# Attention inside a decoder trunk: scores of one query tile ahead of the values of the tile before, and the division by the row sum folded into the transposing product

## The chip, the cores and the metric

The kernel runs on one core of a Trainium2 chip. The metric is the device time of one execution in microseconds, median of several runs. The core has a matrix engine (TensorE: PE for its products, PEld for the loading of its stationary operands), VectorE (DVE), ScalarE (ACT), GpSimd (POOL) and a queue that issues transfers (SyncE, SP).

## What is computed

Two layers of a decoder trunk on 512 tokens of width 1024, in float32: a gated feed-forward half step, a mixer, a second half step, each between a modulated normalisation and a normalised residual. The mixer has three branches beside each other: an attention with 8 heads of 64, a gated linear recurrence (16 blocks of 64) and a matrix-state recurrence (8 heads of 64, called RWKV here). The change lies in the attention branch:

```python
def _fox_attention(q, k, v, f_logit, f_bias):
    log_f = jax.nn.log_sigmoid((f_logit + f_bias).astype(jnp.float32))
    F = jnp.cumsum(log_f, axis=1).transpose(0, 2, 1)
    ...
    def block(args):                       # 128 queries at a time
        qi, Fi, pi = args
        s = jnp.einsum('bhqd,bhkd->bhqk', qi, k).astype(jnp.float32) * scale
        s = s + (Fi[..., :, None] - F[..., None, :])
        s = jnp.where(kpos[None, :] <= pi[:, None], s, -jnp.inf)
        p = jax.nn.softmax(s, axis=-1).astype(v.dtype)
        return jnp.einsum('bhqk,bhkd->bhqd', p, v)
```

## The kernel before

All tokens fit on the chip, so every stage holds 512 columns of tokens and streams weights past them. A weight arrives by one transfer (`raw`, L182), ScalarE rounds it to its leading part (`hi`, L194), GpSimd or VectorE subtracts to get the rest (`lo`, L196), and `mm3` makes three products of the parts (L201 to L203). In the mixer's branch stage (`mix_branches`) GpSimd takes the subtraction.

That stage weaves four generators together. `fox` (attention, four pairs of heads) and then `lru` yield a cost at each step; while the summed cost rises, steps of `rwkv` are taken at a rate of 4 x 30.5 over the whole, gate products (`gates`, L1156 to L1164) up to 22, and background work for the next sub-layer. The steps of `rwkv` are written with a priority 16 instructions ahead of their place. The framework then makes each engine's list: it goes through the program in the order written, by a model of time, and gives an engine the earliest instruction that the model has ready. On the chip an engine takes its list in that order, so an instruction whose input comes later than modelled holds up everything behind it on its engine.

`fox_pair` handles two heads (`hh`) for all tokens. It first makes q, k and v of the pair (L1019 to L1041), then loops over four query tiles `i` of 128 queries. The keys of tile `i` are the first 128(i+1) tokens. For each head: GpSimd adds the causal mask (`fm`, L1052); two products give the scores `sc` (L1054, L1055); VectorE scales, adds the forget bias and keeps the maximum (L1058, and L1062 for the earlier keys), then negates it (`nm`, L1066); ScalarE exponentiates with a row sum (L1068); VectorE takes the reciprocal of the sum (L1069) and multiplies the row by it (L1070). Then, for each head, TensorE transposes `e` block by block into `pt` (L1077), VectorE (head 0, L1082) or ScalarE (head 1, L1080) copies that to `et`, and products with `vs` give the output `po` (L1089), which ScalarE stores to `aout` (L1091). Per pair these are 8 rows of scores and 20 blocks to transpose; over 4 pairs and 2 layers, 64 and 160.

Buffers that matter: `e` has 2 (the tag is shared with `vf` and two tiles of the prelude), `et` 2, and the scores, the transposed blocks, the output and the transposed v share the 3 banks of tag `s` in PSUM.

Of the kernel before, what the change touches and what calls it, by code (L numbers as in the profile page):

```python
# [9 lines left out]
F32 = mybir.dt.float32  # L10
F32R = mybir.dt.float32r
AF = mybir.ActivationFunctionType
ALU = mybir.AluOpType
PSUM = bass.MemoryType.PSUM

P = 128
S = 512
D = 1024
DFF = 2816
NT = S // P  # L20
# [8 lines left out]
H = 8  # L29
# [30 lines left out]
class Trunk:  # L60
# [915 lines left out]
    def fox_prelude(self, l, ap):  # L976

        nc = self.nc
        (w,) = self.raw(self.w_in[:, :, 1536:1568])
        room = ap.tile([P, S], F32, tag="et", bufs=2, name=self.nm("room"))  # L980
        fb = room[:, 5 * NT * H : 5 * NT * H + H]
        nc.scalar.dma_start(out=fb, in_=self.a["fox_f_bias"][l : l + 1, :].broadcast_to([P, H]))
        ps = self.ps("s")

        for k0 in (0, 4):
            for h in (self.hhi, self.hlo):
                for g in range(4):
                    nc.tensor.matmul(out=ps[32 * g : 32 * g + 32, :], lhsT=w[:, k0 + g, :], rhs=h[:, k0 + g, :].bitcast(F32),
                                     start=k0 == 0 and h is self.hhi, stop=k0 == 4 and h is self.hlo, skip_group_check=True)
        yf = ap.tile([P, S], F32, tag="e", bufs=2, name=self.nm("yf"))  # L990
        nc.vector.tensor_copy(yf, ps)
        yield 1.5
        ps = self.ps("s")
        for t in range(NT):
            nc.tensor.matmul(out=ps[:, t * H : (t + 1) * H], lhsT=yf[:, t * P : (t + 1) * P], rhs=self.fold[:, 0:H], start=True, stop=True)
        T = lambda n: room[:, "yezwp".index(n) * NT * H :][:, 0 : NT * H].rearrange("p (t h) -> p t h", t=NT)
        y = T("y")
        nc.vector.tensor_tensor(out=y, in0=ps[:, 0 : NT * H].rearrange("p (t h) -> p t h", t=NT),
                                in1=fb.unsqueeze(1).to_broadcast([P, NT, H]), op=ALU.add)
        sp = self.softplus_neg(y, T)  # L1000
        yield 0.8
        ps = self.ps("s")
        for t in range(NT):
            nc.tensor.transpose(ps[0:H, t * P : (t + 1) * P], sp[:, t, :], self.ident)
        nF = ap.tile([P, S], F32, tag="e", bufs=2, name=self.nm("nF"))[0:H, :]
        ones = self.ones[0:H, :].to_broadcast([H, S])
        nc.vector.tensor_tensor_scan(out=nF, data0=ones, data1=ps[0:H, :], initial=0.0, op0=ALU.mult, op1=ALU.add)
        nc.vector.tensor_scalar(out=nF, in0=nF, scalar1=8.0, scalar2=None, op0=ALU.mult)
        self.nF = self.dp.tile([H, S], F32, tag="nF", bufs=2, name=self.nm("nFd"))
        nc.sync.dma_start(out=self.nF, in_=nF)  # L1010
        yield 0.7

    def fox_pair(self, l, p, ap):


        nc = self.nc
        mm = nc.tensor.matmul


        qs = ap.tile([P, 2, S], F32R, tag="q", bufs=1, name=self.nm("q"))  # L1020
        ks = ap.tile([P, 2, S], F32R, tag="k", bufs=1, name=self.nm("k"))
        kl = self.kl
        vs = ap.tile([P, NT, P], F32, tag="v", bufs=1, name=self.nm("v"))
        ps = self.gemm("aq", p)
        for hh, r in enumerate(ROWS):
            nc.scalar.activation(qs[r, hh, :], ps[r], AF.Copy)
            nc.vector.tensor_tensor(out=qs[ROWS[1 - hh], hh, :], in0=ps[r], in1=qs[r, hh, :].bitcast(F32), op=ALU.subtract)
        yield 5.2
        ps = self.gemm("ak", p)
        for hh, r in enumerate(ROWS):  # L1030
            nc.scalar.activation(ks[r, hh, :], ps[r], AF.Copy)
            nc.vector.tensor_tensor(out=kl[r, hh, :], in0=ps[r], in1=ks[r, hh, :].bitcast(F32), op=ALU.subtract)
            nc.gpsimd.tensor_copy(ks[ROWS[1 - hh], hh, :], ks[r, hh, :])
        yield 5.2
        vf = ap.tile([P, S], F32, tag="e", bufs=2, name=self.nm("vf"))
        nc.vector.tensor_copy(vf, self.gemm("av", p))
        pv = self.ps("s")
        for t in range(NT):
            nc.tensor.transpose(pv[:, t * P : (t + 1) * P], vf[:, t * P : (t + 1) * P], self.ident)
        nc.scalar.activation(vs.rearrange("p t c -> p (t c)"), pv, AF.Copy)  # L1040
        yield 5.2  # L1041
        fbs = []
        for hh in range(2):
            fbs.append(ap.tile([P, S], F32, tag="fb", bufs=2, name=self.nm("fb")))
            nc.sync.dma_start(out=fbs[hh], in_=self.nF[2 * p + hh : 2 * p + hh + 1, :].broadcast_to([P, S]))
        yield 0.9
        for i in range(NT):
            n = i * P
            es = []
            for hh, fb in enumerate(fbs):  # L1050
                fm = ap.tile([P, P], F32, tag="fm", bufs=2, name=self.nm("fm"))
                nc.gpsimd.tensor_tensor(out=fm, in0=fb[:, n : n + P], in1=self.causal, op=ALU.add)  # L1052
                sc = self.ps("s")
                mm(out=sc[:, 0 : n + P], lhsT=qs[:, hh, n : n + P], rhs=ks[:, hh, 0 : n + P], start=True, stop=False)  # L1054
                mm(out=sc[:, 0 : n + P], lhsT=qs[:, hh, n : n + P], rhs=kl[:, hh, 0 : n + P], start=False, stop=True)  # L1055
                e = ap.tile([P, S], F32, tag="e", bufs=2, name=self.nm("e"))
                m = self.sp.tile([P, 2], F32, tag="mx", name=self.nm("mx"))
                nc.vector.tensor_tensor_reduce(out=e[:, n : n + P], in0=sc[:, n : n + P], in1=fm, scale=0.125,  # L1058
                                               scalar=-3e38, op0=ALU.add, op1=ALU.max, accum_out=m[:, 0:1])
                last = m[:, 0:1]  # L1060
                if i:
                    nc.vector.tensor_tensor_reduce(out=e[:, 0:n], in0=sc[:, 0:n], in1=fb[:, 0:n], scale=0.125,  # L1062
                                                   scalar=last, op0=ALU.add, op1=ALU.max, accum_out=m[:, 1:2])
                    last = m[:, 1:2]
                nm = self.sp.tile([P, 1], F32, tag="nmx", name=self.nm("nmx"))
                nc.vector.tensor_scalar(out=nm, in0=last, scalar1=-1.0, scalar2=None, op0=ALU.mult)  # L1066
                rs = self.sp.tile([P, 1], F32, tag="rsum", name=self.nm("rsum"))
                nc.scalar.activation(e[:, 0 : n + P], e[:, 0 : n + P], AF.Exp, bias=nm, accum_out=rs)  # L1068
                nc.vector.reciprocal(rs, rs)  # L1069
                nc.vector.tensor_scalar(out=e[:, 0 : n + P], in0=e[:, 0 : n + P], scalar1=rs, scalar2=None, op0=ALU.mult)  # L1070
                es.append(e)
                yield 0.2 * (i + 1)
            ets = []
            for hh, e in enumerate(es):
                pt = self.ps("s")
                for j in range(i + 1):
                    nc.tensor.transpose(pt[:, j * P : (j + 1) * P], e[:, j * P : (j + 1) * P], self.ident)  # L1077
                et = ap.tile([P, S], F32, tag="et", bufs=2, name=self.nm("et"))
                if hh:
                    nc.scalar.activation(et[:, 0 : n + P], pt[:, 0 : n + P], AF.Copy)  # L1080
                else:
                    nc.vector.tensor_copy(et[:, 0 : n + P], pt[:, 0 : n + P])  # L1082
                ets.append(et)
                yield 0.1 * (i + 1)

            po = self.ps("s")
            for j in range(i + 1):
                for hh, et in enumerate(ets):
                    mm(out=po[64 * hh : 64 * hh + 64, 0:P], lhsT=vs[:, j, hh * 64 : hh * 64 + 64],  # L1089
                       rhs=et[:, j * P : (j + 1) * P], start=j == 0, stop=j == i, skip_group_check=True)  # L1090
            nc.scalar.activation(self.aout[:, p, n : n + P], po[:, 0:P], AF.Copy)  # L1091
            yield 0.25 * (i + 1)

    def mix_branches(self, l):

# [405 lines left out]
```

## Time and profile before

| | |
|---|---|
| median of 3 runs | 3092.01 us (3088.25 to 3103.22) |
| the profiled execution, its own time | 3098.59 us |
| its span, first to last instruction | 3096.5 us |
| PE busy | 2931.2 us, 95% |
| DVE busy | 1880.0 us, 61% |
| ACT busy | 1142.2 us, 37% |
| POOL busy | 554.8 us, 18% |
| mean granted clock of PE | 0.983 |

The attention's query tiles lie from 502 to 782 us of the span in layer 0 and from 2034 to 2313 us in layer 1; between them and after them lie the recurrences, the merge and the feed-forward steps. In the profile, "idle before" an instruction is the time in which its engine did nothing, and the name behind the arrow is what ended that. A row with x4 has four instructions of one line in one piece.

### The profile page before, as it was taken

How to read it: one execution, taken by the hardware profiler on the slowest of the kernel's cores; microseconds unless marked ns; L12 is line 12 of the kernel's file. 1: busy time of each engine (PE TensorE's matmuls, PEld its weight loads, DVE VectorE, ACT ScalarE, POOL GpSimd, SP SyncE). 2: the span in 40 equal slices, each digit the busy share in tenths (PEclk: the TensorE clock that was granted, in tenths of full speed). 3: DMA queues.
4: the chain of work that ended last, by engine and by line, in shares of the span. 5: the costliest groups of instructions: out<-in, count | busy, mean ns of one | idle time of the engine just before them, and what ended most of it. 6: DMA issues, size and time to landing. Idle time of an engine off the chain costs nothing. (4 is left out here: it accounts for less than half of the span.)

```text
span 3096.5 us, 39351 instructions
## 1 busy us (share of the span) xinstructions
PE 2931.2 (95%) x15330; PEld 2338.4 (76%) x15330; DVE 1880.0 (61%) x3534; ACT 1142.2 (37%) x1699; POOL 554.8 (18%) x379
## 2 busy tenths in 40 slices
PE   7999998998989998999999999889989899999998
PEld 5888886676766788888888887767666677788887
DVE  6755567666785656565656546667676756654435
ACT  4322253332545635222342214433335554342212
POOL 0000142333232013000130002423333320230000
PEclk9999999999999999999999999999999999999999
DMA  8634333333342463434434424433333424632221
GB/s 280 224 109 146 115 117 101 88 87 102 94 113 67 139 203 118 139 122 143 129 117 136 133 92 145 127 99 93 88 90 93 107 73 143 204 116 96 89 68 62
DMA packets 389402, 372.17 MB, mean 120 GB/s; under 512 B 54964, under 2 KB 318544, under 8 KB 389216
## 3 DMA queue, kind: packets, MB, share of 16 engines
q1 hardware_dynamic: 377048, 350.14, 37.0%
q10 hardware_dynamic: 12168, 19.53, 1.7%
q8 instruction: 120, 1.97, 0.3%
q14 instruction: 66, 0.54, 0.1%
HBM read 347.54 MB, written 22.09 MB: 119 GB/s over the span
## 5 line engine op out<-in xcount | busy, mean ns | idle before, releaser
L194 ACT ACTIVATE hi<-raw 128x1024 fp32r<-128x1024 f32 (+1 forms) x460 | 469.2, 1028 | 1248.9 <-PE pg L202 501.3
L196 POOL TENSOR_TENSOR lo<-raw,hi 128x1024 fp32r<-128x1024 f32 x164 | 408.0, 2490 | 1692.1 <-ACT hi L194 1639.2
L201 PE MATMUL pg<-hhi,hi 128*128 128x512 f32 (+1 forms) x1744 | 680.4, 393 | 13.7 <-DVE ks L645 3.7
L202 PE MATMUL pg<-hlo,hi 128*128 128x512 f32 (+1 forms) x1744 | 673.5, 389 | 2.9 <-DVE nm L343 2.9
L203 PE MATMUL pg<-hhi,lo 128*128 128x512 f32 (+1 forms) x1744 | 674.8, 391 | 0.0
L196 DVE TENSOR_TENSOR lo<-raw,hi 128x1024 fp32r<-128x1024 f32 (+1 forms) x296 | 342.5, 1165 | 301.3 <-ACT hi L194 296.1
L201 PEld LDWEIGHTS pg<-hhi,hi 128*128 128x128 f32 x1744 | 330.9, 190 | 86.9 <-issue 10.5
L203 PEld LDWEIGHTS pg<-hhi,lo 128*128 128x128 f32 x1744 | 330.6, 190 | 66.5 <-issue 2.1
L202 PEld LDWEIGHTS pg<-hlo,hi 128*128 128x128 f32 x1744 | 331.2, 190 | 65.3 <-issue 4.7
L202 PE MATMUL pr<-hlo,hi 128*128 128x512 f32 (+1 forms) x816 | 300.4, 368 | 5.1 <-DVE nm L343 2.9
L201 PE MATMUL pr<-hhi,hi 128*128 128x512 f32 (+1 forms) x816 | 301.5, 370 | 2.2 <-ACT hhi L397 2.2
L203 PE MATMUL pr<-hhi,lo 128*128 128x512 f32 (+1 forms) x816 | 300.7, 369 | 0.0
L284 DVE SCALAR_TENSOR_TENSOR acc<-raw,cact,acc 128x512 f32<-128x512 f32 x224 | 187.7, 838 | 48.7 <-DMA raw<-in_ada_w_dram 44.3
L202 PEld LDWEIGHTS pr<-hlo,hi 128*128 128x128 f32 x816 | 155.0, 190 | 34.2 <-issue 7.4
L201 PEld LDWEIGHTS pr<-hhi,hi 128*128 128x128 f32 x816 | 155.1, 190 | 28.1 <-ACT hhi L397 2.6
L203 PEld LDWEIGHTS pr<-hhi,lo 128*128 128x128 f32 x816 | 155.2, 190 | 27.4
L352 POOL TENSOR_TENSOR rstd<-var,mhalf 128x1 f32<-128x1 f32 x48 | 30.2, 630 | 470.5 <-DVE var L351 461.9
L201 PE MATMUL ps<-hi,ahi 128*128 128x512 f32 x264 | 103.5, 392 | 0.0
L203 PE MATMUL ps<-hi,alo 128*128 128x512 f32 x264 | 103.3, 391 | 0.0
L202 PE MATMUL ps<-lo,ahi 128*128 128x512 f32 x264 | 103.1, 391 | 0.0
L480 DVE TENSOR_TENSOR su<-pg,su 128x512 f32<-128x512 f32 x42 | 28.9, 689 | 115.2 <-PE pg L203 115.1
L480 DVE TENSOR_TENSOR su<-pr,su 128x512 f32<-128x512 f32 x42 | 29.0, 690 | 110.0 <-PE pr L203 105.9
(443 smaller groups left out, 4956.9 us busy)
## 6 DMA issues: line engine op xcount, KB each, us to landing
raw<-in_ffn_up_dram SPq DMA_DIRECT2D x70, 1024.0 KB
raw<-in_w_in_dram SPq DMA_DIRECT2D x132, 512.0 KB
raw<-in_ada_w_dram SPq DMA_DIRECT2D x64, 1024.0 KB
raw<-in_ffn_down_dram SPq DMA_DIRECT2D x40, 1024.0 KB
raw<-in_ffn_up_dram SPq DMA_DIRECT2D x36, 512.0 KB
gspill<-gate ACTq DMA_DIRECT2D x48, 256.0 KB
gate<-gspill SPq DMA_DIRECT2D x48, 256.0 KB
ada<-in_ada_w_dram SPq DMA_DIRECT2D x16, 512.0 KB
```

What stands on the lines that cost most here:

```text
L194: self.nc.scalar.activation(hi, v, AF.Copy)
L196: eng.tensor_tensor(out=lo, in0=v, in1=hi.bitcast(F32), op=ALU.subtract)
L201: mm(out=ps, lhsT=lhi, rhs=rhi, start=start, stop=False, **kw)
L202: mm(out=ps, lhsT=lhi, rhs=rlo, start=False, stop=False, **kw)
L203: return mm(out=ps, lhsT=llo, rhs=rhi, start=False, stop=stop, **kw).ins
L284: nc.vector.scalar_tensor_tensor(out=acc, in0=r[:, i, :], scalar=c, in1=acc, op0=ALU.mult, op1=ALU.add)
L352: nc.gpsimd.tensor_tensor(out=r, in0=v, in1=self.mhalf, op=ALU.pow)
L480: nc.vector.tensor_tensor(out=su, in0=pss[1], in1=su, op=ALU.mult)
```

## The change

`fox_pair`'s loop over tiles is cut in two generators. `scores(i)` does the work up to the reciprocal, and `values(i)` the rest; they are called in the order scores 0, scores 1, values 0, scores 2, values 1, scores 3, values 2, values 3. The costs that are yielded are the same, in the new order. VectorE no longer multiplies the row by the reciprocal. In its place ScalarE makes a diagonal matrix `dg` from the identity, scaled by the reciprocals, and the transposition of a block by the identity becomes a product of the block with `dg`. `e` gets 4 buffers in place of 2, and `dg` has 4 (6 KB more in each partition).

```diff
-        yf = ap.tile([P, S], F32, tag="e", bufs=2, name=self.nm("yf"))
+        yf = ap.tile([P, S], F32, tag="e", bufs=4, name=self.nm("yf"))
...
-        for i in range(NT):
+        def scores(i, es):
+
             n = i * P
-            es = []
             for hh, fb in enumerate(fbs):
...
                 rs = self.sp.tile([P, 1], F32, tag="rsum", name=self.nm("rsum"))
                 nc.scalar.activation(e[:, 0 : n + P], e[:, 0 : n + P], AF.Exp, bias=nm, accum_out=rs)
                 nc.vector.reciprocal(rs, rs)
-                nc.vector.tensor_scalar(out=e[:, 0 : n + P], in0=e[:, 0 : n + P], scalar1=rs, scalar2=None, op0=ALU.mult)
-                es.append(e)
+                dg = ap.tile([P, P], F32, tag="dg", bufs=4, name=self.nm("dg"))
+                nc.scalar.activation(dg, self.ident, AF.Copy, scale=rs)
+                es.append((e, dg))
                 yield 0.2 * (i + 1)
+
+        def values(i, es):
+
+            n = i * P
             ets = []
-            for hh, e in enumerate(es):
+            for hh, (e, dg) in enumerate(es):
                 pt = self.ps("s")
                 for j in range(i + 1):
-                    nc.tensor.transpose(pt[:, j * P : (j + 1) * P], e[:, j * P : (j + 1) * P], self.ident)
+                    mm(out=pt[:, j * P : (j + 1) * P], lhsT=e[:, j * P : (j + 1) * P], rhs=dg, start=True, stop=True)
...
+        es = [[] for _ in range(NT)]
+        yield from scores(0, es[0])
+        for i in range(NT):
+            if i + 1 < NT:
+                yield from scores(i + 1, es[i + 1])
+            yield from values(i, es[i])
```

## Rows read from the trace of the kernel before

**Rows 1.** The page, part 1: busy time, share of the span, instructions.

```profile
PE 2931.2 (95%) x15330; PEld 2338.4 (76%) x15330; DVE 1880.0 (61%) x3534; ACT 1142.2 (37%) x1699; POOL 554.8 (18%) x379
```

**Rows 2.** Two stretches with attention: PE, PEld, DVE, ACT, POOL busy; clock, DMA.

```profile
477.00:800.00 323.00, 288.70 (x1743) 216.19 (x1742) 223.56 (x625) 107.01 (x216) 98.77 (x79) 0.96 0.34 94
2009.00:2335.00 326.00, 293.46 (x1773) 219.91 (x1773) 228.43 (x628) 112.20 (x224) 101.12 (x79) 0.97 0.35 96
```

**Rows 3.** Waits of PE, 477 to 800: total us, times, longest.

```profile
PE ps L1077 <- DVE e L1070: 14.2, 9, 2.8
PE pr L822 <- DVE room L619: 4.4, 1, 4.4
...
PE ps L1089 <- DVE T L866: 1.0, 1, 1.0
```

**Rows 4.** Waits of PE, 2009 to 2335.

```profile
PE ps L1077 <- DVE e L1070: 11.3, 8, 2.8
```

**Rows 5.** Timeline, layer 0, first pair, tiles 0 and 1: start us, us, engine.

```profile
502.40 0.28 PE L1055 MATMUL ps<-kl,q 128*128 128x128 f32 x1
...
503.28 2.41 POOL L196 TENSOR_TENSOR lo<-raw,hi 128x1024 fp32r<-128x1024 f32 x1 [5.47 <-ACT hi L194]
...
503.49 2.28 DVE L866 TENSOR_TENSOR T<-Y 64x60 f32<-64x60 f32 x1
...
503.88 0.19 ACT L1068 ACTIVATION_READ_ACCUMULATOR e<-e,nmx 128x1 f32 x1
...
506.81 0.15 DVE L1069 RECIPROCAL rsum<-rsum 128x1 f32<-128x1 f32 x1
...
508.25 0.33 PE L1077 MATMUL ps<-ident,e 128*128 128x128 f32 x1 [2.75 <-DVE e L1070]
...
511.76 0.51 PE L1054 MATMUL ps<-k,q 128*128 128x256 f32 x1
```

**Rows 6.** Timeline of one multiplication by the reciprocal and the transposition behind it.

```profile
531.10 2.35 POOL L196 TENSOR_TENSOR lo<-raw,hi 128x1024 fp32r<-128x1024 f32 x1
...
531.36 2.38 DVE L1070 TENSOR_SCALAR e<-e,rsum 128x512 f32<-128x512 f32 x1
...
533.79 0.44 PE L1077 MATMUL ps<-ident,e 128*128 128x128 f32 x2 [1.66 <-DVE e L1070]
```

**Rows 7.** Groups by shape, L1070: busy us, mean ns of one, idle before.

```profile
L1070 DVE TENSOR_SCALAR e<-e,rsum 128x512 f32<-128x512 f32 x16 | 13.3, 831 | 0.1
...
L1070 DVE TENSOR_SCALAR e<-e,rsum 128x128 f32<-128x128 f32 x16 | 8.2, 513 | 0.3
```

**Rows 8.** Stretches behind such waits; columns as in Rows 2.

```profile
508.60:512.00 3.40, 3.40 (x12) 2.10 (x12) 1.89 (x9) 0.38 (x2) 0.00 (x0) 0.50 1.14 304
...
2041.20:2044.60 3.40, 3.40 (x14) 2.33 (x13) 1.64 (x11) 0.55 (x2) 0.00 (x0) 0.50 1.11 281
```

**Rows 9.** Timeline of PE: a run of f32 products, a run of transpositions.

```profile
485.21 1.89 PE L822 MATMUL pr<-AR,KB 128*128 128x256 f32 x8
...
529.49 0.63 PE L1077 MATMUL ps<-ident,e 128*128 128x128 f32 x4 [0.17 <-DVE e L1070]
```

**Rows 10.** Lines L1077, L913: weight loads, min/median/max ns, first and last start.

```profile
L1077 PEld LDWEIGHTS ps<-ident,e x160: 137/140/225, 508.2 to 2308.6; 128*128 128x128 f32 x160
...
L913 PEld LDWEIGHTS pc<-S,AR x224: 186/191/197, 546.0 to 2522.7; 128*128 128x128 f32 x112
```

**Rows 11.** Groups on ACT: busy us, mean ns, idle before and releaser.

```profile
L1091 ACT ACTIVATE aout<-ps 128x128 f32<-128x128 f32 x32 | 8.9, 277 | 42.0 <-PE ps L1089 42.0
```

**Rows 12.** Timeline, the last row sum and its reciprocal.

```profile
2306.50 0.19 ACT L1068 ACTIVATION_READ_ACCUMULATOR e<-e,nmx 128x1 f32 x1
...
2307.01 0.16 DVE L1069 RECIPROCAL rsum<-rsum 128x1 f32<-128x1 f32 x1
```

**Rows 13.** Waits over the whole span.

```profile
ACT UV L924 <- PE pc L922: 107.9, 46, 4.1
...
DVE e L1058 <- PE ps L1055: 40.1, 30, 4.7
```

More of the change, by code (lines that the diff above doesn't have):

```diff
@@ L1004, in fox_prelude @@
             nc.tensor.transpose(ps[0:H, t * P : (t + 1) * P], sp[:, t, :], self.ident)
-        nF = ap.tile([P, S], F32, tag="e", bufs=2, name=self.nm("nF"))[0:H, :]
+        nF = ap.tile([P, S], F32, tag="e", bufs=4, name=self.nm("nF"))[0:H, :]
         ones = self.ones[0:H, :].to_broadcast([H, S])
@@ L1034, in fox_pair @@
         yield 5.2
-        vf = ap.tile([P, S], F32, tag="e", bufs=2, name=self.nm("vf"))
+        vf = ap.tile([P, S], F32, tag="e", bufs=4, name=self.nm("vf"))
         nc.vector.tensor_copy(vf, self.gemm("av", p))
@@ L1055, in fox_pair @@
                 mm(out=sc[:, 0 : n + P], lhsT=qs[:, hh, n : n + P], rhs=kl[:, hh, 0 : n + P], start=False, stop=True)
-                e = ap.tile([P, S], F32, tag="e", bufs=2, name=self.nm("e"))
+                e = ap.tile([P, S], F32, tag="e", bufs=4, name=self.nm("e"))
                 m = self.sp.tile([P, 2], F32, tag="mx", name=self.nm("mx"))
```

## The prediction

> **What bounds the kernel now.** I read the page's busy times first: PE is busy for 95% of the span, no other engine for more than 61% of its own time [rows 1]. So the time is PE's work plus PE's stalls, and a change pays only as far as it takes work or stalls from PE. Next the busy time by stretch: in the two stretches with attention PE works 288.7 of 323 us and 293.5 of 326 [rows 2], so 34.3 and 32.5 us are lost there. Then the waits of PE in these stretches: the largest item is the transposition L1077 waiting for the multiplication L1070, 14.2 us in 9 waits and 11.3 us in 8, 25.5 us together [rows 3, 4]. The other eight of the first stretch (the first and the last stand there) sum to 18.6 us and all wait for VectorE too. Last the timeline of one tile, to see how such a wait comes about. The scores of tile 0 end at 502.68, GpSimd's subtraction runs from 503.28, and a small VectorE step of the RWKV recurrence that starts inside it takes 2.28 us; the row sum is there at 504.07, its reciprocal starts at 506.81, and PE, which has run out of other work placed ahead of it, stands for 2.75 us before the transposition at 508.25 [rows 5]. The multiplication itself is caught in the same way: one beside a subtraction of 2.35 us took 2.38 us, and PE stood 1.66 us for it [rows 6], where 16 of that shape have a mean of 0.83 [rows 7]. The next tile's scores come at 511.76, 9.4 us after those of tile 0 [rows 5]: tile follows tile, and a softmax has only other branches' work to hide behind.
>
> **Waits before the transposing step.** In the new order the products of tile i stand behind the scores of tile i+1. A tile takes 9.4 us from scores to scores here and its softmax 5.8 us from the end of the scores (502.40 + 0.28) to the transposition, wait included [rows 5]. Where the order of writing becomes PE's order, the softmax has ended before its turn comes. But the framework places by readiness in its model: scores 0 and 1 can go at once, as their buffers are free, and values 0 then stand wherever the model sees them ready, as today. Scores 3 also go early (their `e` is free as soon as values 1 are transposed), so values 3 wait for little but values 2. Of the four tiles of a pair, 1 and 2 should be free of waits, and 0 and 3 keep part. Then the multiplication is gone from the chain, so a stretched one can't stop PE in any tile; ten of 64 were over 1.4 us (the one of [rows 6] is the first), and 10.8 us of the 25.5 stand behind these ten. That leaves 14.7 us behind late maxima and reciprocals. If tiles 0 and 3 keep most of their share, some 6.5 us remain: 25.5 - 6.5 = 19 us gained. Bounds: 10.8 (only the stretched multiplications) and 25.5 + 2 x 1.0 (the wait of L1089, [rows 3]; one like it lies in layer 1) = 27.5.
>
> **Clock.** Behind four of these waits lie stretches with a granted clock of 0.50, 1.2 in place of 2.4 GHz: 508.6 to 512.0 after the idle time that ends at 508.25, and 2041.2 to 2044.6 after the same wait in layer 1 are the first and the last [rows 5, 8]; the other two (from 744.1 and 771.5) follow waits of 2.58 and 1.55 us. PE is busy all through such a stretch [rows 8], so half of 3.4 us is lost each time: 4 x 1.7 = 6.8 us. A stretch goes when its wait goes; with 19 of 25.5 us I take 4 us. Bounds 0 and 6.8.
>
> **TensorE.** 160 transpositions become 160 products of the same size. A run of eight f32 products of 256 columns has starts (1.89 - 0.38) / 7 = 0.216 us apart, 0.108 for 128 columns; four transpositions of 128 are (0.63 - 0.27) / 3 = 0.12 apart [rows 9]. So the product itself costs nothing more. Its weight load takes 190 ns where a transposition's takes 140 [rows 10], but it runs beside the product before it. I take 0; if all were exposed, 160 x 0.05 = 8 us more.
>
> The Trainium skill (FP8 and Floating Point Precision, TensorE Precision Notes) speaks against the change: true FP32 takes four passes through the array. [rows 9] don't bear out that a product would cost four times a transposition; the time by that rule is the fifth case below.
>
> **VectorE.** 64 multiplications go: 13.3 us in the widest of four shapes and 8.2 in the narrowest [rows 7], 39.9 us over the four, 20 us a layer of the 224 and 228 that VectorE works in these stretches [rows 2], 9% of it. The other waits for VectorE are 18.6 us in the first stretch; a proportional share would be 1.7 us a layer. Most of them come at q, k, v or the recurrences, away from the softmax, so I take 1 us in all; bounds 0 and 8 (a stretched multiplication in VectorE's line delays what is behind it by 1.5 to 2 us as well).
>
> **ScalarE.** 64 diagonals come: the nearest row is a 128x128 copy with 277 ns [rows 11], 64 x 0.28 = 18 us. New is that ScalarE waits for the reciprocal: its line is held from the row sum to the reciprocal's end. That was 2.74 us to the reciprocal's start for the first pair of instructions [rows 5] and 0.32 for the last [rows 12]; over all 64 pairs the mean is 0.57, 37 us. Queued behind are the rounding of weights (L194), gate values (L1163), `et` and `aout`, and the recurrence's copy UV (L924), whose products PE needs next. In the stretches ScalarE works 107 of 323 us [rows 2], and L924 itself waits for PE 107.9 us in the span [rows 13], so most of the 18 + 37 = 55 us hides there. I take 2 us on PE; bounds 0 and 55 (all of it passed on).
>
> **What else moves.** `fm` on GpSimd and the maxima on VectorE come a tile earlier; no transfer is moved past another, since the bias rows are loaded before the loop and the stores stay. Scores i+1 hold two of the three `s` banks until VectorE has read them, so the second head's products may wait for that. VectorE sat waiting for the scores in 30 of 64 cases [rows 13], so it reads them at once about half the time. I take 0; if 24 tiles waited 1 us each it would be 24. The buffers (6 KB) cost no time; the yielded costs keep the pace of the other branches.
>
> **Sum.** -19 - 4 - 1 + 2 = -22 us. The profiled execution, 3098.6 (span 3096.5 and 2.1 around it), would become 3076.6. It lies 6.6 us above the median of the runs, 3092.0, so the forecast is 3092 - 22 = 3070.
>
> **The rivals.**
> 1. *The forecast*, 3070, own range 3052 to 3082 (gain 40 to 10): PE idle before L1077 is the largest stall, and two of its sources are removed.
> 2. *Only the multiplication counts*: the planner puts the products just where its model has them ready, as now, and VectorE's lateness hits them again. Gain 10.8, less 2 for ScalarE, plus 2 of clock: 3081. For it: transpositions already stand in the middle of other products. Against: the products of tiles 1 and 2 have been ready long before in any model.
> 3. *New waits take all*: the `s` banks, 24 us, against 22: 3094. For it: VectorE reads scores as late as the recurrence lets it. Against: the 30 waits of [rows 13].
> 4. *ScalarE is held* (the slower side): an in-order line that waits for a VectorE that may be 2.7 us late [rows 5]; the recurrence's copies queue behind it. Price 55 us times the share that reaches PE. Against a gain of 24 without that term it decides from 24 / 55 = 44% on; with three quarters passed on, 3092 - 24 + 41 = 3109.
> 5. *The f32 product costs four transpositions*: 160 x 3 x 0.108 = 52 us on PE, 3122. Against it: [rows 9].
>
> **How the numbers follow.** Chances: forecast 0.55, only the multiplication 0.20, new waits 0.14, ScalarE 0.08, product 0.03. The likeliest gives 3070. About 0.5% (15 us) is what a measurement of this kernel can tell from no change, so faster means below 3076.5: most of the first case (0.47), a quarter of the second and some of the third, 0.55. Slower means above 3107.5: most of the last two, 0.09. The same: 0.36. The range for 8 in 10 goes from 3050 (a gain of 42: the upper bounds of waits, clock and VectorE, 27.5 + 6.8 + 8) to 3100, which takes in the second and third case and leaves out most of the last two.
>
> **What would show it.** In the new trace the waits of PE before the product line should sum to 4 to 10 us, not 25; half-clock stretches after 508, 771 and 2041 should be gone; VectorE should be busy 40 us less and ScalarE 18 more; starts in a run of these products should be 0.11 us apart. Wrong would be: waits of the products for the `s` banks (VectorE's L1058 or L1062), L924 or L194 waiting for the reciprocal and PE waiting for them, or products 0.4 us apart. The forecast fails also if the idle time only moves to the next VectorE step, as the recurrence's.

## The result and the profile after

The change makes the kernel slower: 3126.85 us median against 3092.68, a ratio of 1.0112 (95% interval 1.0081 to 1.0143). The forecast was 3070 with a range of 3050 to 3100. The profiled execution took 3135.54 us with a span of 3133.8, 37.3 more than before's.

Busy times of after, page part 1 (before: [rows 1]):

```profile
PE 2963.9 (95%) x15490; PEld 2361.0 (75%) x15490; DVE 1860.5 (59%) x3470; ACT 1161.4 (37%) x1763; POOL 554.7 (18%) x379
```

PE works 32.7 us more, in 160 more instructions. VectorE works 19.5 us less and ScalarE 19.2 more.

The whole branch stage, from the first low-rank product of the recurrence (L704) to the first product of the merge, in both layers. First before, then after; columns as in [rows 2]:

```profile
459.00:1039.30 580.30, 527.63 (x3139) 395.33 (x3137) 392.85 (x949) 253.66 (x430) 175.94 (x119) 0.97 0.34 93
1990.60:2572.00 581.40, 529.95 (x3140) 396.91 (x3138) 392.55 (x949) 253.71 (x430) 174.43 (x118) 0.97 0.34 92
```

```profile
459.20:1058.20 599.00, 547.75 (x3219) 410.24 (x3218) 381.70 (x917) 262.89 (x462) 175.37 (x119) 0.96 0.33 90
2007.40:2606.40 599.00, 545.66 (x3219) 409.40 (x3217) 382.83 (x917) 262.93 (x462) 176.40 (x119) 0.97 0.32 90
```

The stage is 18.7 and 17.6 us longer, and that is 36 of the 37 us. PE's idle time in it (length less busy) is 52.7 and 51.5 us before, 51.3 and 53.3 after: it hasn't moved. PE's busy time has grown by 20 and 16 us.

The products with the diagonal, line L1082 of after, min/median/max ns:

```profile
L1082 PEld LDWEIGHTS ps<-dg,e x320: 186/192/333, 510.3 to 2334.6; 128*128 128x128 f32 x160
L1082 PE MATMUL ps<-dg,e x320: 270/275/436, 510.5 to 2334.7; 128*128 128x128 f32 x160
```

One run of them in the timeline of PE (start and length in us):

```profile
514.36 1.05 PE L1082 MATMUL ps<-dg,e 128*128 128x128 f32 x8
```

160 products are 320 instructions: each is issued twice, each time with its own weight load of 192 ns. Eight starts lie (1.05 - 0.28) / 7 = 0.11 us apart, so a product takes 0.22 us where a transposition took 0.11 (the median of 90 starts in the trace of before; the run of four in [rows 9] has 0.12). That is 160 x 0.11 = 18 us, nine a layer.

The waits of PE in the stage of layer 0, after (total us, times, longest; of 21 lines the first three, and the largest of the attention's query tiles):

```profile
PE pr L756 <- DVE rw L753: 5.7, 3, 3.1
PE pg L201 <- DVE rst L333: 4.8, 1, 4.8
PE pr L808 <- DVE KT L813: 4.6, 1, 4.6
...
PE ps L1054 <- DVE mx L1058: 3.3, 2, 3.1
PE ps L1094 <- DVE et L1087: 3.2, 2, 2.1
...
PE ps L1082 <- ACT dg L1071: 2.6, 3, 1.8
```

The wait ahead of the transposing step fell from 14.2 us [rows 3] to 2.6 as forecast. The waits that grew or came stand at the recurrences, at products for want of a PSUM bank, at the scores and at the values. One of them, from the timelines of VectorE, GpSimd and PE in after:

```profile
868.06 2.36 DVE L330 TENSOR_SCALAR rsq<-rst 128x8 int32<-128x8 int32 x1
...
868.02 2.37 POOL L196 TENSOR_TENSOR lo<-raw,hi 128x1024 fp32r<-128x1024 f32 x1 [2.55 <-ACT hi L194]
...
872.89 0.75 DVE L1248 SCALAR_TENSOR_TENSOR xc<-pg,vcol,xc 128x509 f32<-128x509 f32 x1
...
873.78 0.76 PE L201 MATMUL pg<-hhi,hi 128*128 128x512 f32 x1 [4.80 <-DVE rst L333]
```

A step on eight columns starts just behind GpSimd's subtraction and ends with it, 2.36 us long; the line before it, on the same shape, takes 0.17. The three steps L1248 that free the bank come that much later, and PE stands for 4.80 us. It is the picture of [rows 5] with another victim. It is also the rule: in the stage of layer 0 of before all 39 instructions of VectorE that are over 0.5 us longer than the shortest of their line and shape run beside a subtraction on GpSimd, and each ends 0.02 to 0.55 us behind the end of that.

What else makes PE busier is the clock and the mixture. The stretches with a granted clock of 0.50 sum to 30.7 and 34.1 us in the stages of before, 44.4 and 37.5 in after. A split product (one of the three of `mm3`, of parts rounded to fp32r) of 512 columns starts 0.43 us behind the one before it there and 0.23 us elsewhere, so nearly half of the 17 us more is lost, 8. And PE's list changes between the split products and f32 work some 400 times a stage before, some 460 after. What a change costs, in two timelines of PE in before:

```profile
541.96 0.40 PE L202 MATMUL pg<-hlo,hi 128*128 128x512 f32 x1
542.20 0.40 PE L203 MATMUL pg<-hhi,lo 128*128 128x512 f32 x1
542.52 0.44 PE L922 MATMUL pc<-UX,Q 64*64 64x64 f32 x4
...
546.01 0.39 PE L202 MATMUL pg<-hlo,hi 128*128 128x512 f32 x1
546.24 0.55 PE L913 MATMUL pc<-S,AR 128*128 128x64 f32 x4
546.73 0.45 PE L916 MATMUL pc<-UV,AM 128*64 128x64 f32 x4
```

The first pair of numbers in a row is the rows and columns of the array in use. It is 0.24 us from split product to split product and 0.32 to the first f32 product on 64*64, but 0.23 to an f32 product on 128*128 (L913). So the 0.09 us belongs to the step from the whole array to a part of it; the way back costs about as much (0.15 us in the median from a product on a part to a split product, where two of the part follow each other at 0.05 to 0.06). Transpositions and products with the diagonal use the whole array. Of steps between the whole array and a part there are 308 in a stage of before and 332 in after: 24 x 0.09 = 2 us a layer, 4 in both. Products 18, clock 8, steps 4: 30 of the 36 us by which PE is busier, with idle time at nothing. The other 6 are not placed.

### The profile page after: what moved, and what is told of

Its sections match the earlier page's. It is cut to its first block, busy times and chain, and to the rows that moved or that the text cites. A ratio compares the mean times of both kernels' runs of the same rounds, so it can differ in the third digit from the quotient of the medians.

```text
span 3133.8 us, 39681 instructions
## 1 busy us (share of the span) xinstructions
PE 2963.9 (95%) x15490; PEld 2361.0 (75%) x15490; DVE 1860.5 (59%) x3470; ACT 1161.4 (37%) x1763; POOL 554.7 (18%) x379
## 5 line engine op out<-in xcount | busy, mean ns | idle before, releaser
L201 PEld LDWEIGHTS pg<-hhi,hi 128*128 128x128 f32 x1744 | 333.1, 191 | 92.4 <-issue 20.3
L284 DVE SCALAR_TENSOR_TENSOR acc<-raw,cact,acc 128x512 f32<-128x512 f32 x224 | 171.8, 767 | 42.6 <-DMA raw<-in_ada_w_dram 37.9
```

Source lines behind the costliest of these rows:

```text
L201: mm(out=ps, lhsT=lhi, rhs=rhi, start=start, stop=False, **kw)
L284: nc.vector.scalar_tensor_tensor(out=acc, in0=r[:, i, :], scalar=c, in1=acc, op0=ALU.mult, op1=ALU.add)
```

## The experiments

Three numbers of each profile stand in a table: PE's idle time in the branch stage of layer 0, and VectorE's *stretched* instructions there. I call one stretched that is over 0.5 us longer than the shortest of its line and shape; behind the count is the time by which they exceed it. The expectations count one or two more.

| kernel | ratio to before (95%) | stage, us | PE idle, us | stretched |
|---|---|---|---|---|
| before | 1 | 580 | 52.7 | 39, 64 us |
| after | 1.0112 (1.0081 to 1.0143) | 599 | 51.3 | 38, 62 |
| e1 product alone | 1.0072 (1.0052 to 1.0093) | 593 | 53.1 | 42, 67 |
| e2 order alone | 1.0061 (1.0044 to 1.0078) | 591 | 54.1 | 40, 68 |
| e3 diagonal, old order | 1.0049 (1.0030 to 1.0069) | 588 | 44.3 | 32, 51 |
| e4 order, ScalarE divides | 1.0070 (1.0047 to 1.0094) | 595 | 56.2 | 40, 68 |
| e5 order, in one block | 1.0073 (1.0055 to 1.0092) | 591 | 56.7 | 39, 68 |
| e6 old order, tiles yield nothing | 1.0212 (1.0195 to 1.0229) | 618 | 69.6 | 43, 73 |
| e7 old order, ScalarE divides | 0.9965 (0.9952 to 0.9978) | 571 | 45.7 | 38, 59 |
| e8 no division | 1.0042 (1.0026 to 1.0058) | 584 | 52.1 | 36, 61 |
| e9 old order, other pace | 1.0005 (0.9994 to 1.0016) | 585 | 52.4 | 40, 65 |
| e10 order, other pace | 1.0037 (1.0025 to 1.0049) | 586 | 49.4 | 36, 64 |
| e11 old order, VectorE splits | 0.9675 (0.9650 to 0.9701) | 532 | 17.2 | 4, 3 |
| e12 order, VectorE splits | 0.9627 (0.9609 to 0.9645) | 521 | 12.3 | 5, 5 |
| e13 after, VectorE splits | 0.9709 (0.9694 to 0.9724) | 532 | 10.8 | 4, 4 |
| e14 as e12, ScalarE divides | 0.9614 (0.9598 to 0.9629) | 517 | 9.6 | 5, 4 |
| e15 diagonal, VectorE splits | 0.9683 (0.9667 to 0.9698) | 529 | 9.9 | 5, 4 |
| e16 as e12, no split on GpSimd | 0.9610 (0.9593 to 0.9627) | 520 | 11.8 | 5, 5 |
| e17 product, VectorE splits | 0.9692 (0.9674 to 0.9710) | 529 | 11.3 | 5, 4 |
| e18 e14 and e16 together | 0.9574 (0.9556 to 0.9592) | 517 | 9.7 | 5, 4 |

**e1, the product alone**, in the kernel before:

```diff
-  nc.tensor.transpose(pt[...], e[...], self.ident)
+  mm(out=pt[...], lhsT=e[...], rhs=self.ident, start=True, stop=True)
```

> The kernel before with one edit: each transposition is written as a product with the identity. Division on VectorE and order as before. Theory A (the product is what costs: the trace of after has 320 instructions for 160 products, some 0.106 us apart, where before had 160 instructions 0.109 us apart): 160 x 0.106 = 17 us more, about 3109 us, 1.0055 of before, give or take 4. Theory B (the new order alone costs the 34 us, by turning the planner's lists over): 0, about 3092.

Measured: 3118.82 us against 3094.3, by the ratio 22 us more (16 to 29). Line L1077 of e1 (min/median/max ns):

```profile
L1077 PE MATMUL ps<-ident,e x320: 270/275/554, 510.0 to 2325.5; 128*128 128x128 f32 x160
```

The stage of layer 0 in e1, columns as in [rows 2]:

```profile
459.40:1052.50 593.10, 539.96 (x3219) 406.51 (x3217) 395.17 (x949) 253.31 (x430) 174.04 (x119) 0.97 0.33 91
```

The second instruction is there with nothing else changed, and PE works 12 us more in the stage at the same idle time. Theory B is out; theory A's 17 us lie inside the interval, at its lower end.

**e2, the order alone**: after with L1070 and the transposition of before in their places.

> The order of after (scores of the next tile ahead of values, four buffers of e), but the division stays on VectorE and the blocks are transposed as before. Theory A: the waits before the transposition go (up to 25 us), but changes between kinds of products (some 50 more per layer in the trace of after, about 0.09 us each, 10 us) and waits at later VectorE steps take most of it back: 3092, between 3080 and 3102. Theory B: 34 us more, about 3126.

Measured: 3113.41, 19 us more (14 to 24): between the theories and outside both. PE's waits in the stage of layer 0 of e2 (total us, times, longest):

```profile
PE pr L844 <- DVE T L881: 5.6, 2, 3.0
PE pr L756 <- DVE rw L753: 5.4, 2, 3.0
PE pg L201 <- DVE rst L333: 4.8, 1, 4.8
...
PE ps L1081 <- DVE e L1070: 2.3, 1, 2.3
```

The same stage of e2, columns as in [rows 2]:

```profile
458.40:1049.40 591.00, 536.94 (x3140) 398.12 (x3139) 393.90 (x949) 252.12 (x430) 173.73 (x118) 0.97 0.33 91
```

The transposition (L1081 here) waits 2.3 us for L1070 in place of 14.2 (and 1.6 more for late maxima), and PE still idles 54 us.

**e3, the diagonal alone**, in the loop of before.

> The order of before, two buffers of e; the diagonal of reciprocals on ScalarE and the product with it as in after. Theory A: 17 us more for the products, 11 us less for the stretched multiplications: 3098, between 3090 and 3110. Theory B: 11 us less and 2 more for ScalarE: 3083. Theory C (ScalarE held by the reciprocal): over 3110, with PE waiting for the recurrence's copies.

Measured: 3109.71, 15 us more (9 to 21), inside theory A's range at its upper end. Together with e2 that is 34 us, what after costs: the halves add, within their intervals. The 7 us by which e3 stands under e1 are no more than the intervals. In its profile PE idles 8 and 9 us less in the two layers than before, with 32 stretched instructions in place of 39, and more of its time goes at half clock (the granted clock of its runs is 0.981, of before 0.984).

**e4, the order with the division on ScalarE**:

```diff
-  nc.vector.tensor_scalar(out=e[...], in0=e[...], scalar1=rs, scalar2=None, op0=ALU.mult)
+  nc.scalar.activation(e[...], e[...], AF.Copy, scale=rs)
```

> The order of after; ScalarE multiplies the rows by the reciprocal in place of VectorE (same pass over the row), and the blocks are transposed as before. Theory A: like the order alone, with 40 us of VectorE's work gone and no second pass on PE: 3083, between 3070 and 3095. Theory B: 3126. Theory C (ScalarE's line held): 3110 or more here too.

Measured: 3114.82. VectorE's relief buys nothing in this order; there are 40 stretched instructions, as in e2. The time lies in the range of theory C, but the order alone takes the same with VectorE dividing, and PE waits only 2.8 us in the whole span for ScalarE's rows: a held line of ScalarE isn't seen.

**e5 and e6, fewer yields.** In e5 the order of after is kept, the inner yields go, and a tile yields its whole cost once:

```diff
-        yield from scores(0, es[0])
+        done = sum(scores(0, es[0]))
...
-                yield from scores(i + 1, es[i + 1])
-            yield from values(i, es[i])
+                done += sum(scores(i + 1, es[i + 1]))
+            done += sum(values(i, es[i]))
+            yield done
```

e6 was to do the same in the order of before. Its edit takes the three yields out and puts none in their place:

```diff
-                yield 0.2 * (i + 1)
...
-                yield 0.1 * (i + 1)
...
-            yield 0.25 * (i + 1)
```

So a pair's four tiles are written in one piece, and their 8.5 units of cost a pair are never counted, 34 of the 193.2 by which the other branches are paced. The last steps of the matrix-state recurrence are left for the end: its last product at L967 starts at 1063 us of the trace, behind the last product of the linear recurrence with `whi` (1020), where in before it starts ahead of that (1005 and 1029).

> The order of after with division on VectorE and transpositions (as in the order alone, which took 0.61% more than before), but a tile's yields are drawn together: scores of the next tile and values of this one are written without other branches' steps between them, and the cost is yielded once a tile. PE's list then changes between f32r products and f32 work 910 times, where the order alone has 1002 and before 894. Theory S (the changes between kinds and the stretches of half clock that come with a scattered list are what the order costs): within 0.2% of before, 3088 to 3100. Theory O (the order as such, because scores and values in flight hold banks and VectorE): 3110 to 3116, as the order alone.

> The order, division and transpositions of before, with a tile's yields drawn together to one at its end. PE's list changes kind 994 times in place of 894. Theory S: 100 more changes at about 0.09 us are 9 us, and half-clock stretches may add to that: 3103 to 3113. Theory O: no change of order, so 3090 to 3098.

Measured: 3114.56 and 3159.25. With 910 changes of kind e5 stays at the order's time, so the number of changes doesn't decide, and theory S fell. e6 tests neither theory, since its edit isn't the one that its expectation describes; its 65 us are the price of a pace that leaves the attention out. PE idles 69.6 us there, most at the recurrences, and the granted clock is 0.972; the longest waits of PE in the stage of layer 0 of e6 (total us, times, longest):

```profile
PE pr L967 <- DVE Yt L963: 15.9, 4, 5.5
PE pg L201 <- DVE xc L1232: 10.0, 3, 4.3
```

**e7, ScalarE divides in the old order; e8, no division** (the division by the row sum is left out).

> The order of before; ScalarE multiplies the rows by the reciprocal in place of VectorE, blocks transposed as before (918 changes of kind). If the stretched multiplications on VectorE cost the 7 us by which the diagonal (15 us more) stands under the product alone (22 us more): about 3087. If idle time only moves to the next late VectorE step: 3094. If ScalarE's line held by the reciprocal costs: 3100 or more.

> The kernel before without the multiplication by the reciprocal: the division by the row sum is left out, nothing takes its place (910 changes of kind). It bounds what any cheaper division can bring in the order of before. If the waits at the transposition are a loss by themselves: 10 to 25 us less, 3070 to 3084. If PE's idle time is set by what else VectorE and GpSimd owe (idle time was 51 to 54 us per layer in before, after and the order alone): under 8 us less, 3086 or more.

Measured: 3082.19, 11 us less, and 3106.42, 13 us more. e8 takes work and a link of the chain away and is slower. What PE waits there ahead of the transposition, in the stage of layer 0:

```profile
PE ps L1076 <- ACT e L1068: 5.3, 4, 2.3
```

That is 5.3 us in place of 14.2, and PE's idle time is that of before (52.1 us and 50.8 in the two layers, 52.7 and 51.5 before). So in this list the waits at the transposition weren't a sum to be cashed. The 13 us are for the most part clock: the granted clock of e8's runs is 0.9815 on average and that of before's beside them 0.9849. The difference is 0.0034 of 3100 us, at the loss read above some 10 us (an estimate). e7 shows the other side: in layer 0 PE waits 3.6 us for ScalarE's rows in place of 14.2, and its idle time falls by 7 us there and by 5 in layer 1.

**e9 and e10, another pace.** How much is only a list laid otherwise?

```diff
-  yield 0.2 * (i + 1)
+  yield 0.225 * (i + 1)
...
-  yield 0.25 * (i + 1)
+  yield 0.2 * (i + 1)
```

> The kernel before with the yielded costs of a tile shared out a little otherwise (0.225 in place of 0.2 for each row of scores, 0.2 in place of 0.25 for the values; the sum is the same). No work changes; the planner's lists do, a little. It measures how far a list that is only laid otherwise moves the time. Theory N (a new list moves the time by up to 0.7% either way, so that the order's 0.61% and the 0.42% of the kernel without division are of that kind): anything between 3072 and 3115, outside 0.2% of before. Theory P (lists that differ this little take the same time, and the order costs by its own mechanism): 3088 to 3100.

> The order of after with division on VectorE and transpositions, with the same shift of the yielded costs. Theory N: anything between 3080 and 3135. Theory P: as the order alone, 3108 to 3119.

Measured: 3097.39 (2 us more) and 3106.04 (11 us more). A small shift of the list moves the old order by nothing and the new one by 8 us. So with GpSimd's split the order costs, 11 to 23 us over e2, e5 and e10, but its size hangs on the list: set beside the old order with the same edit it is 9 us at the other pace (e10 against e9) and 32 with ScalarE's division (e4 against e7).

**e11 and e12, the split on VectorE.** In the table so far idle time goes with the stretched instructions more than with the softmax. So GpSimd's subtraction leaves the branch stage, under the old order and the new:

```diff
-  self.wide, self.on_pool = False, True
+  self.wide, self.on_pool = False, False
```

> The kernel before; in the branch stage the subtraction for the split of weights is on VectorE in place of GpSimd. Over all kernels so far PE's idle time in the stage goes with the time that VectorE's instructions lose beside a subtraction on GpSimd (before: 40 stretched instructions and 65 us lost a layer, PE idle 52; the diagonal alone: 33, 53 and 43). Theory L (these stretched instructions make PE's idle time, wherever the softmax stands): stretched instructions fall to a few, PE's idle time falls below 40 us a layer, unless VectorE's own load (some 90 us more a layer on 439 of 580) takes their place. Theory M (PE idles for the chains of the softmax and the recurrence themselves): idle stays above 50 us or grows with VectorE's load; 3110 or more.

> The order of after with division on VectorE and transpositions; the subtraction on VectorE as in the run before it. Theory L: without stretched instructions the order gains what the prediction expected of it, 5 to 20 us against the run before it. Theory N or P: it stands some 19 us above the run before it, as with GpSimd.

Measured: 2994.57 and 2980.24, against the same runs of before. The old order gains 3.25%, and here the new order is 14 us *faster* than the old, the intervals apart. Page part 1 of e12:

```profile
PE 2889.6 (97%) x15330; PEld 2311.0 (78%) x15330; DVE 1882.2 (63%) x3662; ACT 1140.6 (38%) x1699; POOL 255.4 (9%) x251
```

Its stage in layer 0, columns as in [rows 2]:

```profile
458.60:980.10 521.50, 509.25 (x3140) 385.21 (x3138) 388.06 (x1003) 252.95 (x430) 48.94 (x63) 1.00 0.37 101
```

PE's longest waits in that stage of e12 (total us, times, longest):

```profile
PE pg L201 <- ACT gate L1175: 2.2, 2, 1.4
PE pr L808 <- ACT UV L802: 1.8, 1, 1.8
PE ps L1266 <- DVE xs L1252: 1.5, 2, 0.8
```

VectorE takes 54 more instructions in the stage and is busy 388 us where it was 393: the time that it lost beside GpSimd paid for all of them. PE idles 12 us in place of 53, the clock is 1.00, and no single wait is over 2 us. Of the 115 us that e12 gains, 80 are idle time of PE in the two stages. The Trainium skill (SBUF — State Buffer, "SBUF: two separate sides") calls the port pair of GpSimd and VectorE an exclusive lock, held for the whole instruction; the 39 stretched steps of before, which end just behind GpSimd's subtraction, agree with it.

**e13 to e17.** What was left open: does each half of the change behave so? The edits are those above, together with the split on VectorE; e16 takes the split off GpSimd in the feed-forward stages too.

> The kernel after, with the subtraction of the branch stage on VectorE. Theory L (order gains where nothing is stretched beside GpSimd; the product costs two instructions): 2980 of the order with VectorE, plus 17 to 22 for the products, less a few for VectorE's 40 us: 2994, between 2988 and 3002. If the product's price was mostly waiting, under 2985.

> The order of after with transpositions, the row multiplied by the reciprocal on ScalarE, and the subtraction of the branch stage on VectorE. VectorE has 40 us less to do than in the order with VectorE (2980) and ScalarE 35 us more. Theory L: 2970 to 2980. If ScalarE's line held by the reciprocal costs: 2985 or more.

> The order of before with the diagonal and the product, and the subtraction of the branch stage on VectorE. Theory L: no stretched multiplication is left to be saved, so the whole price of the product shows: 2994.6 + 17 to 22 = 3012 to 3017. If the 7 us that the diagonal gave back with GpSimd came from VectorE's load alone: 3005 to 3010.

> The order with division and all subtractions on VectorE, in the first chunk of the feed-forward stages too (there GpSimd had some 40 of its 164 subtractions). If stretched instructions cost PE time there as well: 2965 to 2975. If PE has enough placed ahead in that stage: 2977 to 2984, as the order with VectorE in the branch stage alone.

> The order and division of before, each transposition as a product with the identity, the subtraction of the branch stage on VectorE. If the product costs its second instruction wherever it stands: 2994.6 + 17 to 22 = 3012 to 3017, and the diagonal's other half gives some 19 us back. If the product is free with VectorE's subtractions: 2990 to 2998.

Measured: 3001.08, 2972.23, 2992.91, 2969.53, 2998.11. After (e13) stands 21 us above the order without the product (e12), 25 by the ratios, and 29 above e14, which was run beside it and divides on ScalarE too: the product's price shows in full, as in e1. e14 and e16 came as expected. e15 and e17 missed: by the ratios to before the products cost 2 us in the old order with the diagonal and 5 with the multiplication on VectorE, each give or take some 9, where 17 to 22 were forecast. PE's idle time says where it went: 17.2 us a layer in e11, 11.3 in e17, 9.9 in e15. PE's extra work fills time in which it stood; under the new order there are only 12.3 us to fill, and after uses 1.5 of them. That also turns the order's sign: with the products, e13 stands 8 us above the old order (e15), where without them e12 stands 14 below it (e11).

**e18, what the runs point to**: the new order, transpositions, the division on ScalarE, no split on GpSimd in any stage.

> The order of after with transpositions, the row multiplied by the reciprocal on ScalarE, and no weight's subtraction on GpSimd in any stage. The parts alone gave 2972 (ScalarE, GpSimd in the feed-forward stage) and 2970 (VectorE's multiplication, no GpSimd) against 2980: if they add, 2962; if they meet the same waits, 2969 to 2972.

Measured: 2962.23 us, 4.26% less than before and 5.3% less than after. The medians add (8 and 11 us alone, 18 together); by the ratios it is 4 and 5 alone and 16 together, with intervals of some 5 us on each, so the sum is not sharp.

## Why the prediction was wrong

**TensorE, taken at 0 with a bound of 8 us.** This step failed first: 18 us by the rows, 22 in e1. I divided a run of eight by eight products. The count of a row is of instructions, and the rows of before told so, in the groups by shape:

```profile
L822 PE MATMUL pr<-AR,KB 128*128 128x256 f32 x128 | 38.5, 447 | 16.4 <-DVE room L619 8.7 <-DVE AR L778 7.7
L1089 PE MATMUL ps<-et,v 128*64 128x128 f32 x320 | 37.8, 294 | 2.0 <-DVE T L866 2.0
```

The program writes 64 products at L822 and 160 at L1089; the transpositions at L1077 have 160 instructions for 160. A count held against the program would have given two instructions a product and 18 us. The fifth case, at 0.03, was the nearest in mechanism, and it priced four transpositions where two were due. Split products of 512 columns start 0.23 us apart, 0.058 for 128 columns; the f32 product's 0.22 is four times that, and a transposition's 0.11 is twice that. The rule that I set aside (the Trainium skill, FP8 and Floating Point Precision, TensorE Precision Notes: four passes for true FP32) agrees with the trace when it is held against a split product; I had held it against a transposition.

**Waits before the transposing step, 19 us.** The local forecast held: 2.6 us are left in layer 0 and 2.1 in layer 1, 4.7 in all, within the 4 to 10 named. That this is a gain was the second step to fail. PE's idle time stayed (52.7 and 51.5 us before, 51.3 and 53.3 after), and e2 and e8 show it without the product: the wait ends and another late VectorE step is next. The last sentence of the prediction names that, but no rival priced it; the third put it at the `s` banks with 24 us, and PE waits 6.9 us for those in the whole span (L1054 for L1058). Its lower bound was read a little high: 10.5 us, not 10.8, stand behind the ten stretched multiplications. I had seen both stretched steps [rows 5, 6] and put them down to the softmax's chain rather than to GpSimd's 176 us a stage beside a VectorE that works 393 of 580.

**Clock, -4 us.** It went the other way, +8: the stages of after have more time at half clock, and one such stretch still lies in the first tile, from 506.4 us. Why they fall where they do isn't shown.

**VectorE, 40 us less.** 19.5 by the page: 64 multiplications went, but the stretched time stayed (64 us and 62 in layer 0) and fell on other instructions. **ScalarE, +2.** A diagonal takes 0.40 us in place of 0.28, and ScalarE waits for the reciprocal 20.3 us in 31 cases; PE waits 4.7 us for diagonals. The held line was no large cost, and the fourth case, the slower side of the forecast, isn't what happened.

**The sum.** Forecast -22; measured +34. The product explains 18 to 22 of the 56 between them. The rest is a gain of 24 that didn't come, and about 10 besides, close to the 8 of the clock.

**What is shown and what isn't.** Shown: the product's price (e1, e13; in e15 and e17 PE's idle time takes it up), the order's cost under GpSimd's split (e2, e5, e10), the stretch of VectorE's steps beside GpSimd and what moving the split gains (e11, e12), and that PE's idle time can stay when the wait ahead of the transposition goes (e2, e8). Not shown: that the order is at a loss *because* of the stretched instructions. e11 and e12 speak for it; e13 and e15, where the order costs 8 us with few of them, speak against it. Moving the split also gives the planner other lists and the low parts sooner; that alone wasn't tried. But all eight kernels with VectorE's split idle 10 to 17 us in the stage, whatever else stands in their lists, and no list of PE's waits has one for the low parts. Of e2's 19 us the clock of its runs (0.982 in place of 0.984) makes some 6 by the same estimate, the 24 steps more a layer between the whole array and a part of it 4, and idle time 3. The rest, and why the new order spends more time at half clock, stays open.

## What to carry to other kernels

When one engine's stalls all end with the same late engine, ask what makes that engine late before taking one of the stalls away: the wait moves to the next step, and only the cause (here a neighbour that holds VectorE up) was worth its sum. Count a line's instructions against the operations that the program writes before taking a pitch from a run of them. And when an edit turns a planned list over, run the edit's halves and an edit that changes nothing but the pace beside it, and keep the sum of the costs that pace it: e6 dropped them, and measured that.

## What the runs showed that was not expected

- An f32 product of 128 columns is two instructions with two weight loads, 0.22 us; a transposition of the same block is one, 0.11.
- Moving 54 subtractions of 1.17 us a stage from GpSimd (2.4 us each) to VectorE left VectorE's busy time where it was (393 and 388 us) and took 3.25% off the kernel.
- Taking the multiplication out altogether (e8) made the kernel 0.42% slower; moving it to ScalarE (e7) made it 0.35% faster.
